# Taking the 512 token columns of a matmul in another order: runs of 4 to 128 columns, alternating between two halves

## The chip, the cores and the metric

The kernel runs on one core of a Trainium2 chip. A core has a matrix engine (TensorE, PE in the profile, with its weight loads listed apart as PEld), VectorE (DVE), ScalarE (ACT), GpSimd (POOL) and SyncE (SP, which issues the DMAs here). Matmuls read their operands from SBUF and write sums into PSUM, which has banks of 512 fp32 columns for each of 128 partitions. The metric is the device time of one execution in microseconds; less is better.

## The reference

A streaming encoder of two layers on one sequence of 512 tokens and 1,024 features, all fp32:

```python
def swiglu(h, w_in, w_out):
    gate, up = jnp.split(h @ w_in, 2, axis=-1)
    return (jax.nn.silu(gate) * up) @ w_out

def reference(x, ...):
    for l in range(DEPTH):                       # DEPTH = 2
        x = x + 0.5 * swiglu(rms_norm(x, ffn1_norm[l]), ffn1_w_in[l], ffn1_w_out[l])
        x = x + hybrid_mixer(rms_norm(x, mix_norm[l]), ...)
        x = x + 0.5 * swiglu(rms_norm(x, ffn2_norm[l]), ffn2_w_in[l], ffn2_w_out[l])
    return rms_norm(x, final_norm)
```

`w_in` is 1024 x 5632 (gate and up), `w_out` is 2816 x 1024. The mixer is a projection, three groups of heads (a convolution, stick-breaking attention, retention) and a projection back. The change concerns only the last product of `swiglu`, here called the outward product.

## The kernel before

Activations lie feature-major: a tile is 128 features (partitions) by 512 tokens (columns), so `x` is eight tiles. A weight block of 128 x 128 is the stationary operand of a matmul, a tile of activations the moving one, and the result, 128 output features by 512 tokens, fills one PSUM bank.

To keep fp32 accuracy each operand is split into a rounded part and a rest, `hi` and `lo`, both of type fp32r. Weights arrive by DMA (`w_raw`), ScalarE casts them (L347) and VectorE subtracts (L350). `product` (L357 to L374) then makes three matmuls for each block of 128 input features: hi x hi (L368), hi x lo (L369) and lo x hi (L370), all summed into one bank `acc`. `self.pe` puts two blocks, six matmuls, into one step of the plan.

`ffn` handles the 2,816 hidden features as 22 tiles in three parts, `PARTS` = tiles 0 to 7, 8 to 15 and 16 to 21. For each hidden tile of a part it makes the gate sums `pg` and the up sums `pu` (eight blocks each, so 24 matmuls each), and `gated` turns them into the split pair `hh`, `hl` on VectorE and ScalarE (L476 to L480, L315, L318). When a part's tiles are there, the outward products run: for each of the eight output tiles d, `po` sums over the part's 8, 8 or 6 hidden tiles, so 24, 24 or 18 matmuls. VectorE scales `po` into `t` (L502) and adds that to `x[d]` (L507). Over the four FFNs each output tile d takes 4 x 22 x 3 = 264 outward matmuls.

The order on every queue comes from a planner. Each step is given a cost (for a group of matmuls the number of columns times `COLUMN`), a list of what it reads and writes and, in the mixer, a delay. The planner plays all engines forward in time and writes the steps out in the order in which they start. So outward products of one part stand among the first gate and up products of the next. PSUM has three banks for `pg`, `pu`, `po` and the projections.

One product elsewhere matters for reading the profile. In the stick-breaking heads `scores` adds a mask to the diagonal blocks of a bank of scores. Where the bank holds two such blocks it does so in one matmul, whose output is a view of two pieces and whose moving operand is the same 128 columns twice (L655):

```python
diag = z[:].rearrange("p (a b) -> p a b", b=P)[:, 0 : 3 * n - 2 : 3, :]
mm(
    diag, self.ident_r[:], self.mask[:, None, :].to_broadcast([P, n, P]), start=False, stop=True,
```

The retention heads run the same `scores` without the mask. `weighted` (L676) multiplies weights with values in plain slices of 512, 384, 128 and 256 columns, and `values` (L607 to L609) makes value tiles in plain slices of 512 or 256 columns; the values are then written to SBUF in pieces of 64 columns, hi and lo in turn (L621, L625).

Of the kernel before, what the change touches and what calls it, by code (L numbers as in the profile page):

```python
# [27 lines left out]
N_RAW = 3  # L28

DENSE_LATE, TAPS_LATE = 200, 400  # L30
PARTS = ((0, 8), (8, 16), (16, 22))
TT = S // P

# [42 lines left out]
class Plan:  # L76
# [167 lines left out]
    def order(self):  # L244
        self.link()
        self.total = self.forward([o.i + o.late for o in self.ops])
        return sorted(self.ops, key=lambda o: (o.start, o.i))
# [42 lines left out]
class Kernel:  # L290
# [63 lines left out]
            )  # L354
        return hi, lo

    def product(self, acc, w, rhs, ks, first=True, last=True, step=2):  # L357

        mm = self.nc.tensor.matmul
        hi, lo = w  # L360
        for a in range(0, len(ks), step):
            some = ks[a : a + step]

            def fn(a=a, some=some):
                for i, (k, m) in enumerate(some):
                    c = slice(k * P, (k + 1) * P)
                    h, l = rhs[m]
                    mm(acc[:], hi[:, c], h[:], start=first and a + i == 0, stop=False)  # L368
                    mm(acc[:], hi[:, c], l[:], start=False, stop=False)  # L369
                    mm(acc[:], lo[:, c], h[:], start=False, stop=last and a + i == len(ks) - 1)  # L370

            self.pe(
                len(some) * 3 * S * COLUMN, fn, [hi, lo, *(t for _, m in some for t in rhs[m])], [acc], self.late
            )  # L374
# [94 lines left out]
    def ffn(self, w_in, w_out, after, first=None):  # L469
        nc = self.nc  # L470
        ks = [(k, k) for k in range(KT)]

        def gated(pg, pu, hs):
            rstd = self.rstd
            g, s, u = (self.tile(self.f2, n) for n in "gsu")
            self.v(S, lambda: nc.vector.tensor_tensor(out=g[:], in0=pg[:], in1=rstd[:], op=ALU.mult), [pg, rstd], [g])  # L476
            self.last_silus = [
                self.a(S, lambda: nc.scalar.activation(s[:], g[:], ACT.Silu), [g], [s], "silu")
            ]
            self.v(S, lambda: nc.vector.tensor_tensor(out=u[:], in0=pu[:], in1=s[:], op=ALU.mult), [pu, s], [u])  # L480
            self.split(u, S, *hs)

        pg, pu = self.products(first or [self.weight(w_in[0, i], KT) for i in range(2)], self.mm)
        self.norm(self.y)
        for a, b in PARTS:
            n = b - a
            hs = [(self.tile(self.r2, "hh", dtype=F32R), self.tile(self.r2, "hl", dtype=F32R)) for _ in range(n)]
            for f in range(a, b):
                if f:
                    pg = self.bank(self.mm, "pg")  # L490
                    self.product(pg, self.weight(w_in[f, 0], KT), self.xs, ks)
                    pu = self.bank(self.mm, "pu")
                    self.product(pu, self.weight(w_in[f, 1], KT), self.xs, ks)
                gated(pg, pu, hs[f - a])
            for d in range(KT):
                po = self.bank(self.mm, "po")
                self.product(po, self.weight(w_out[d][:, a:b, :], n), hs, ks[:n])
                t = self.tile(self.f2, "t")
                x, rstd = self.x[d], self.rstd
                self.v(  # L500
                    S,
                    lambda t=t, po=po, rstd=rstd: nc.vector.scalar_tensor_tensor(  # L502
                        out=t[:], in0=po[:], scalar=0.5, in1=rstd[:], op0=ALU.mult, op1=ALU.mult
                    ),
                    [po, rstd], [t],
                )
                self.v(S, lambda t=t, x=x: nc.vector.tensor_tensor(out=x[:], in0=x[:], in1=t[:], op=ALU.add), [x, t], [x], 2)  # L507
                if b == NF:
                    after(d)
# [641 lines left out]
```

## Time and profile before

| what | value |
|---|---|
| time, median of two runs | 2012.01 us (2010.58 to 2013.43) |
| the profiled execution's own time | 2009.54 us |
| its span, first to last instruction | 2007.7 us |
| PE busy | 1955.3 us (97%), 8,930 matmuls |
| DVE busy / ACT busy | 1094.5 us (55%) / 753.6 us (38%) |
| mean granted TensorE clock | 0.991 |
| outward matmuls `po` | 3 groups (L368, L369, L370) of 704 |

Spans, busy times and waits are those of one profiled execution. A group's row gives its busy time, the mean duration of one instruction in ns, and the idle time of its engine just before it, with what ended that idle time. Matmuls overlap in the pipeline, so the duration of one is longer than its distance to the next.

### The profile page before, as it was taken

The page shows a single profiled execution, that of the slowest core. Times are in us where ns is not written, and L with a number is a line of the kernel's source. Part 1 is how long each engine was busy: PE and PEld are TensorE (multiplying, and loading weights), DVE is VectorE, ACT ScalarE, POOL GpSimd, SP SyncE. Part 2 cuts the span into 40 slices and gives each one's busy share as a digit, 9 for nine tenths or more (in the row PEclk, how much of TensorE's full clock was granted, in tenths as well). Part 3 has the DMA queues.
Part 4 walks back from the last instruction along what each step waited for, and adds up shares of the span by engine and source line. Part 5 has one row for each costly group of instructions (what it writes and reads, how often), then busy time and mean ns, then how long its engine had stood idle before and what let it go on. Part 6 is the DMA issues. An engine that isn't in the chain of part 4 may idle for free.

```text
span 2007.7 us, 22494 instructions
## 1 busy us (share of the span) xinstructions
PE 1955.3 (97%) x8930; PEld 1619.5 (81%) x8930; DVE 1094.5 (55%) x1505; ACT 753.6 (38%) x1096; POOL 20.3 (1%) x21
## 2 busy tenths in 40 slices
PE   8999999999988999999999999999999799999997
PEld 6888888888867888888888888888887588888885
DVE  5443433768996444444643444456699954444445
ACT  5322223564955322223422222236559543222132
POOL 0000000000000000000000000000000000000000
PEclk9999999999999999999999999999999899999998
DMA  6323232432213232332323323223321133233221
GB/s 206 101 90 104 85 104 77 125 94 90 58 42 105 86 104 95 94 104 84 98 95 98 101 94 104 90 78 117 94 85 51 49 111 96 93 105 95 95 89 58
DMA packets 60777, 187.95 MB, mean 94 GB/s; under 512 B 8320, under 2 KB 8832, under 8 KB 60544
## 3 DMA queue, kind: packets, MB, share of 16 engines
q1 hardware_dynamic: 60672, 186.52, 29.8%
q8 instruction: 70, 1.15, 0.2%
q14 instruction: 35, 0.29, 0.0%
HBM read 176.00 MB, written 2.10 MB: 89 GB/s over the span
## 4 chain that ended last, share of the span: by engine, by line
PE 76%; issue 18%; DVE 4%; ACT 1%; DMA 0%; POOL 0%; SPq 0%; POOLq 0%; DVEq 0%; ACTq 0%
PE po L369 6%; PE po L370 6%; PE po L368 6%; PE pu L368 6%; PE pg L370 6%; PE pg L369 6%; PE pu L369 6%; PE pg L368 6%; PE pu L370 6%; PE pj L368 3%; PE pj L370 3%; PE pj L369 3%; PE z L726 2%; DVE yc L890 1%; PE z L648 1%
## 5 line engine op out<-in xcount | busy, mean ns | idle before, releaser
L347 ACT CAST w_hi<-w_raw 128x1024 fp32r<-128x1024 f32 (+2 forms) x354 | 349.5, 989 | 1027.8 <-PE po L369 298.6
L350 DVE TENSOR_TENSOR w_lo<-w_raw,w_hi 128x1024 fp32r<-128x1024 f32 (+2 forms) x354 | 402.0, 1143 | 42.0 <-ACT w_hi L347 31.4
L480 DVE TENSOR_TENSOR u<-pu,s 128x512 f32<-128x512 f32 x84 | 58.1, 692 | 491.3 <-PE pu L370 491.3
L370 PE MATMUL po<-hh,w_lo 128*128 128x512 f32 x704 | 273.9, 389 | 0.0
L369 PE MATMUL po<-hl,w_hi 128*128 128x512 f32 x704 | 273.9, 389 | 0.0
L368 PE MATMUL po<-hh,w_hi 128*128 128x512 f32 x704 | 273.9, 389 | 0.0
L368 PE MATMUL pg<-xh,w_hi 128*128 128x512 f32 x672 | 263.2, 392 | 0.0
L368 PE MATMUL pu<-xh,w_hi 128*128 128x512 f32 x672 | 261.6, 389 | 0.1
L370 PE MATMUL pg<-xh,w_lo 128*128 128x512 f32 x672 | 261.5, 389 | 0.0
L369 PE MATMUL pg<-xl,w_hi 128*128 128x512 f32 x672 | 261.4, 389 | 0.0
L370 PE MATMUL pu<-xh,w_lo 128*128 128x512 f32 x672 | 261.4, 389 | 0.0
L369 PE MATMUL pu<-xl,w_hi 128*128 128x512 f32 x672 | 261.4, 389 | 0.0
L502 DVE SCALAR_TENSOR_TENSOR t<-po,rstd 128x512 f32<-128x512 f32 x96 | 66.3, 691 | 202.4 <-PE po L370 202.3
L368 PEld LDWEIGHTS po<-hh,w_hi 128*128 128x128 f32 x704 | 132.2, 188 | 27.5
L369 PEld LDWEIGHTS po<-hl,w_hi 128*128 128x128 f32 x704 | 132.2, 188 | 27.5
L370 PEld LDWEIGHTS po<-hh,w_lo 128*128 128x128 f32 x704 | 132.1, 188 | 27.3
L369 PEld LDWEIGHTS pg<-xl,w_hi 128*128 128x128 f32 x672 | 126.2, 188 | 27.1 <-issue 1.0
L368 PEld LDWEIGHTS pu<-xh,w_hi 128*128 128x128 f32 x672 | 126.1, 188 | 27.1 <-DVE g L476 0.9
L368 PEld LDWEIGHTS pg<-xh,w_hi 128*128 128x128 f32 x672 | 126.2, 188 | 27.0 <-issue 1.0
L369 PEld LDWEIGHTS pu<-xl,w_hi 128*128 128x128 f32 x672 | 126.2, 188 | 26.2
L370 PEld LDWEIGHTS pg<-xh,w_lo 128*128 128x128 f32 x672 | 126.1, 188 | 26.1
L370 PEld LDWEIGHTS pu<-xh,w_lo 128*128 128x128 f32 x672 | 126.2, 188 | 26.1
(149 smaller groups left out, 2565.0 us busy)
## 6 DMA issues: line engine op xcount, KB each, us to landing
w_raw<-in_f_in SPq DMA_DIRECT2D x174, 512.0 KB, 3.3
w_raw<-in_f_out SPq DMA_DIRECT2D x64, 512.0 KB, 3.5
w_raw<-in_m_in SPq DMA_DIRECT2D x36, 512.0 KB, 3.4
w_raw<-in_f_out SPq DMA_DIRECT2D x32, 384.0 KB, 3.1
w_raw<-in_m_out SPq DMA_DIRECT2D x32, 256.0 KB, 3.0
w_raw<-in_m_vs SPq DMA_DIRECT2D x8, 512.0 KB, 3.4
qh<-qh SPq DMA_DIRECT2D x24, 128.0 KB, 2.2
ql<-ql SPq DMA_DIRECT2D x24, 128.0 KB, 2.8
```

Source lines behind the costliest of these rows:

```text
L347: self.a(m, lambda c=c: nc.scalar.copy(hi[:, c], raw[:, c]), [at(raw)], [at(hi)])
L350: lambda c=c: nc.vector.tensor_tensor(out=lo[:, c], in0=raw[:, c], in1=hi[:, c].bitcast(F32), op=ALU.subtract),
L368: mm(acc[:], hi[:, c], h[:], start=first and a + i == 0, stop=False)
L369: mm(acc[:], hi[:, c], l[:], start=False, stop=False)
L370: mm(acc[:], lo[:, c], h[:], start=False, stop=last and a + i == len(ks) - 1)
L480: self.v(S, lambda: nc.vector.tensor_tensor(out=u[:], in0=pu[:], in1=s[:], op=ALU.mult), [pu, s], [u])
L502: lambda t=t, po=po, rstd=rstd: nc.vector.scalar_tensor_tensor(out=t[:], in0=po[:], scalar=0.5, in1=rstd[:], op0=ALU.mult, op1=ALU.mult),
L648: mm(z[:, c : c + n], k[:, kt * P : (kt + 1) * P], q[i][:, kt * P :], start=kt == tiles[0][0] and i == 0, stop=end and i == 1,)
L726: nc.tensor.matmul(z[:, c : c + n], m[:], logs[jb][part][:, jc : jc + n], start=False, stop=i == len(todo) - 1 and part == 1, skip_group_c ...
L890: nc.vector.scalar_tensor_tensor(out=y[:], in0=v, scalar=w, in1=y[:], op0=ALU.mult, op1=ALU.add)
```

## The change

`product` gets an argument `turns`. With 1, the operands are whole tiles as before. With b > 1, the output bank and both moving operands are passed as the same rearranged view of 512 columns: the columns are cut into two halves (tokens 0 to 255 and 256 to 511), each half into pieces of b columns, and the view takes a piece of the first half, a piece of the second, the next piece of the first and so on. As output and moving operand are taken in the same order, each token's result stands in the column where it stood before. `ffn` passes `TURNS[d]` for the outward products alone, by output tile: 1 for tile 0, then 4, 8, 16, 32, 64, 128 and, for tile 7, 16.

```diff
+TURNS = (1, 4, 8, 16, 32, 64, 128, 16)
...
-    def product(self, acc, w, rhs, ks, first=True, last=True, step=2):
+    def product(self, acc, w, rhs, ks, first=True, last=True, step=2, turns=1):
...
+        def order(t):
+            return t[:] if turns == 1 else t[:].rearrange("p (a n b) -> p n a b", a=2, b=turns)
...
-                    mm(acc[:], hi[:, c], h[:], start=first and a + i == 0, stop=False)
-                    mm(acc[:], hi[:, c], l[:], start=False, stop=False)
-                    mm(acc[:], lo[:, c], h[:], start=False, stop=last and a + i == len(ks) - 1)
+                    mm(order(acc), hi[:, c], order(h), start=first and a + i == 0, stop=False)
+                    mm(order(acc), hi[:, c], order(l), start=False, stop=False)
+                    mm(order(acc), lo[:, c], order(h), start=False, stop=last and a + i == len(ks) - 1)
...
-                self.product(po, self.weight(w_out[d][:, a:b, :], n), hs, ks[:n])
+                self.product(po, self.weight(w_out[d][:, a:b, :], n), hs, ks[:n], turns=TURNS[d])
```

## The prediction
> **What bounds the kernel now.** I read the page of the profile first, for the engine that is never free.
>
> ```profile
> span 2007.7 us, 22494 instructions
> ...
> PE 1955.3 (97%) x8930; PEld 1619.5 (81%) x8930; DVE 1094.5 (55%) x1505; ACT 753.6 (38%) x1096; POOL 20.3 (1%) x21
> ...
> PE   8999999999988999999999999999999799999997
> ...
> PEclk9999999999999999999999999999999899999998
> ```
>
> TensorE is busy for 97% of the span. Its slices fall under 9 only at the start, around slices 12 and 32 (the ends of the two mixers) and at the very end, and the granted clock is at 0.9 or more in all slices but one. VectorE and ScalarE have 45% and 62% of the span to spare. Busy PE time alone doesn't say that the array is the limit, so the second view is the busy time of each engine in four stretches that hold the outward products `po`, the only instructions that the change touches.
>
> ```profile
> core 0: us, PE busy (x) PEld busy (x) DVE busy (x) ACT busy (x) POOL busy (x), PEclk, DMA share, GB/s
> 96.00:140.00 44.00, 44.00 (x195) 36.44 (x195) 19.86 (x25) 9.02 (x10) 0.00 (x0) 1.00 0.33 100
> 335.00:376.00 41.00, 41.00 (x182) 33.94 (x181) 29.33 (x42) 20.24 (x29) 0.00 (x0) 1.00 0.34 104
> 1846.00:1890.00 44.00, 44.00 (x196) 36.44 (x195) 20.26 (x25) 9.20 (x10) 0.00 (x0) 1.00 0.27 84
> 1953.00:1990.00 37.00, 37.00 (x165) 30.56 (x163) 20.39 (x30) 9.73 (x15) 0.00 (x0) 1.00 0.16 43
> ```
>
> In all four PE is busy for the whole stretch at clock 1.00, and no other engine is over 83% (PEld) or 72% (DVE). The third view is the groups by line.
>
> ```profile
> L370 PE MATMUL po<-hh,w_lo 128*128 128x512 f32 x704 | 273.9, 389 | 0.0
> L369 PE MATMUL po<-hl,w_hi 128*128 128x512 f32 x704 | 273.9, 389 | 0.0
> L368 PE MATMUL po<-hh,w_hi 128*128 128x512 f32 x704 | 273.9, 389 | 0.0
> ...
> L502 DVE SCALAR_TENSOR_TENSOR t<-po,rstd 128x512 f32<-128x512 f32 x96 | 66.3, 691 | 202.4 <-PE po L370 202.3
> L368 PEld LDWEIGHTS po<-hh,w_hi 128*128 128x128 f32 x704 | 132.2, 188 | 27.5
> ```
>
> No `po` product ever found PE idle (0.0 in the last column of all three). VectorE, which takes `po` out of PSUM, is the one that waits: 202.3 us for PE. The weight load takes 188 ns and then has a gap, 27.5 us over 704 loads or 39 ns each, so 227 ns from one load to the next.
>
> The mean of 389 ns is a latency, since neighbours overlap. What a product costs is the distance between starts. From the order of time in the first FFN, these are the first and the last of 1,059 starts of `pg`, `pu` and `po` products in a row.
>
> ```profile
> 100.13 0.39 PE L368 MATMUL pu<-xh,w_hi 128*128 128x512 f32 x1
> ...
> 339.95 0.39 PE L370 MATMUL pu<-xh,w_lo 128*128 128x512 f32 x1
> ```
>
> 239.82 us over 1,058 distances is 226.7 ns per product, with `po` and `pu` alike. So every nanosecond added to a `po` product is added to the span, and nothing hides it.
>
> **The change part by part.** *What is touched.* 704 x 3 = 2,112 `po` products, 264 for each of the eight output tiles. Tile 0 has a turn of 1 and stays as it is. The other seven are 1,848 products, at 226.7 ns together 418.9 us, a fifth of the span.
>
> *What is added.* Each of them still writes 512 columns and reads 512 columns, in another order: pieces of b columns, one from tokens 0 to 255, one from 256 on, in turn. That is 512/b pieces in place of one run, 128, 64, 32, 16, 8, 4 and 32 for the tiles 1 to 7, so 127 + 63 + 31 + 15 + 7 + 3 + 31 = 277 jumps over the seven, each with 264 products: 73,128 jumps, on the reading side (h, l in SBUF) and the writing side (`po` in PSUM) at once.
>
> *What stays.* No instruction comes or goes and no wait is added. The output goes through the same order as the input, so each token's sum stands in its own column, and VectorE reads `po` as a plain row as before. The planner is given the same cost for each group, so the orders of all queues (weight loads on SP, casts on ScalarE, subtractions on VectorE) are the same list. All of this costs nothing even without cover, since it doesn't change.
>
> *What a jump costs* is the one unknown. The trace has one matmul form with a jump: the mask product of the stick-breaking heads (L655), whose 256-column form writes two pieces of 128 columns, 0 to 127 and 384 to 511 of a bank, and reads the same 128 columns twice, so that reading jumps too. It stands behind two 128-column products on the same bank. In the retention heads, which have no mask, a plain 256-column product stands at the same place. First the masked head, then the plain one, each with the product before and the one behind:
>
> ```profile
> 517.00 0.27 PE L648 MATMUL z<-ql,kk 128*128 128x128 f32 x1
> 517.11 0.33 PE L655 MATMUL z<-r_mask,ident_r 128*128 128x256 f32 x1
> 517.28 0.39 PE L368 MATMUL pj<-xh,w_hi 128*128 128x512 f32 x1
> ```
>
> ```profile
> 444.65 0.27 PE L648 MATMUL z<-ql,kk 128*128 128x128 f32 x1
> 444.76 0.33 PE L648 MATMUL z<-qh,kk 128*128 128x256 f32 x1
> 444.94 0.28 PE L648 MATMUL z<-ql,kk 128*128 128x256 f32 x1
> ```
>
> Start to start, the product with the jump takes 0.17 us, the one without 0.18. Over all such, from the groups by line with shapes kept apart (the `y` product also follows two 128-column ones; the `pv` rows are wanted for the columns):
>
> ```profile
> L608 PE MATMUL pv<-w_hi,xl 128*128 128x512 f32 x64 | 25.0, 390 | 0.0
> ...
> L608 PE MATMUL pv<-w_hi,xl 128*128 128x256 f32 x64 | 18.1, 283 | 0.0
> ...
> L676 PE MATMUL y<-wh,vs 128*128 128x256 f32 x16 | 5.4, 334 | 0.0
> ...
> L655 PE MATMUL z<-r_mask,ident_r 128*128 128x256 f32 x16 | 5.3, 332 | 0.0
> ```
>
> 332 against 334 ns: one jump costs -2 ns, nothing within what the rows resolve, and I take 2 ns either way as the bound. Upward that is 73,128 x 2 ns = 146 us. Downward a better limit holds: the `pv` rows give (390 - 283)/256 = 0.418 ns per column, so 512 columns need 214.0 of the 226.7 ns, and an order of columns can at best win the other 12.7 ns: 1,848 x 12.7 = 23.5 us.
>
> Pieces under 128 columns don't occur on PE in this trace. The nearest rows are VectorE's, which writes `vs` in pieces of 64 (every other 64 columns of SBUF) and `xl` as a plain row with the same operation:
>
> ```profile
> L398 DVE SCALAR_TENSOR_TENSOR xl<-x,c_gains,xh 128x512 fp32r<-128x512 f32 x48 | 35.6, 748 | 7.1 <-ACT xh L395 7.0
> ...
> L625 DVE SCALAR_TENSOR_TENSOR vs<-pv,rt,vs 128x512 fp32r<-128x512 f32 x8 | 6.0, 746 | 1.3 <-ACT vs L621 1.3
> ```
>
> 746 against 748 ns with seven jumps: no price for a jump on that side either, though on a slower engine. Between 0 and 2 ns per jump I take 0, the value that both pairs of rows are nearest to.
>
> *The sum*: 1,848 x 0 ns on the path, nothing elsewhere. The profiled execution took 2009.5 us with a span of 2007.7; the two timed runs have a median of 2012.0, 2.5 us above it. I forecast 2,011 us, between the two.
>
> The Trainium skill has two rules on this. PSUM — Partial Sum Buffer, section Specifications (TRN2), says of PSUM's 8-byte lines that any access pattern that isn't contiguous slows matmuls significantly; the mask product above isn't contiguous and doesn't show it, and if the rule held in that form the time would be the one of the third rival. Advanced Engine Details and Errata, section Memory Cachelines, asks less: two accesses to each 16-byte line of SBUF and each two neighbouring columns together in PSUM, which pieces of 4 fp32 columns satisfy, so by that section the sum stays as it is; no run here shows pieces that short on PE.
>
> **The rivals.** *1. Each jump costs a little.* The pair of rows resolves 2 ns, but a price of one column's time, 0.418 ns, would slip under it, and 73,128 x 0.418 = 30.6 us gives about 2,041 us. Two columns' time, 0.836 ns, is 61.1 us, 2,072 us. For: the jumps are many and PE has no slack. Against: both pairs came out at -2 ns, and 334 ns would have become 334.4, which they can't deny. It turns to slower by over 2% (40 us) at 0.55 ns per jump. I give 0.05 to the part below that point and 0.08 to the part above.
>
> *2. Only the shortest pieces cost (the rival on the slow side with one place).* Pieces of 4 columns (tile 1, 264 products) lie 256 columns apart, so that a fetch of a few neighbouring columns serves one piece and the next fetch goes elsewhere. If such a product ran at half the pace, 264 x 226.7 ns = 59.8 us, 2,071 us; if pieces of 8 did as well, 119.7 us, 2,131 us. It decides from a pace of 1.67 times in tile 1 (40 us). For: nothing under 128 was seen. Against: four columns still lie side by side. Chance 0.08.
>
> *3. Any break halves the pace.* All 1,848 products at 453 ns: 418.9 us, about 2,430 us. Against it stands the mask product, broken and no slower; what is left is that a break in reading to a far column, or a third free dimension, counts and that one didn't. Chance 0.04. This is the rule of PSUM — Partial Sum Buffer in the Trainium skill, taken at its word.
>
> *4. The order helps.* Up to 23.5 us, so 1,987 to 2,009 us. No row speaks for it. Chance 0.02.
>
> That the change doesn't do what it says is hardly possible: with two halves in turn no two pieces are neighbours, so the rows can't be merged back into one.
>
> **How the numbers follow.** No change has 0.73. That case alone spans 2,003 to 2,017 us: the profiled run and the two timed ones lie within 4 us, and I allow twice that. The range reaches from 2,003 to 2,042 us, which takes in the first rival up to one column's time per jump (0.05) and part of the fourth, about 0.8 in all; the 2 ns bound is left out, since its upper half would need a price that the mask product should have shown. Chances by 2% either side, about what a measurement of this kernel can tell from no change: slower 0.08 + 0.08 + 0.04 = 0.20; faster 0.01, since the limit of 23.5 us is 1.2%; within 2% the remaining 0.79.
>
> **What would show it right or wrong.** The distance between starts is the whole test. In the third part of each FFN (335 us on in the first) the eight tiles follow one another with 18 products each, so about 4.1 us of `po` for each piece length. If all eight show 226.7 ns, the main step holds. If the distance grows with the number of jumps, about in the ratio 127, 63, 31, 15, 7, 3, the first rival holds; if only tile 1 stretches, the second; if all but tile 0 stretch alike, the third. VectorE's wait for `po` (202.3 us) should stay if PE keeps its pace and grow if it doesn't. A changed granted clock, or PE idle before `po`, would mean that something happened that I didn't consider.

## The result, and the profile after

The changed kernel took 2,037.41 us (median of two runs, 2,036.81 to 2,038.02) against 2,012.01: a ratio of 1.0126 [1.0083, 1.017], so it is slower by about 25 us, inside the forecast range and within 2%, but beyond what the runs scatter. The page of the changed kernel, its head and the shares by engine:

```profile
span 2035.0 us, 22504 instructions
...
PE 1982.5 (97%) x8930; PEld 1625.8 (80%) x8930; DVE 1096.1 (54%) x1505; ACT 754.2 (37%) x1096; POOL 20.3 (1%) x21
...
PEclk9999999999999999999999999999999899999998
```

The span grew by 27.3 us (2,035.0 against 2,007.7) and PE's busy time by 27.2 (1,982.5 against 1,955.3), with as many matmuls and the other engines within 2 us. The time is all on PE. The groups by line say in which products (lines stand six further down than before; the last numbers of a row are busy us, mean ns, idle us before and its releaser):

```profile
L375 PE MATMUL po<-hl,w_hi 128*128 128x512 f32 x704 | 281.6, 400 | 0.0
L376 PE MATMUL po<-hh,w_lo 128*128 128x512 f32 x704 | 281.5, 400 | 0.0
L374 PE MATMUL po<-hh,w_hi 128*128 128x512 f32 x704 | 281.1, 399 | 0.0
...
L508 DVE SCALAR_TENSOR_TENSOR t<-po,rstd 128x512 f32<-128x512 f32 x96 | 66.3, 691 | 222.3 <-PE po L376 221.3
```

The three groups of `po` hold 844.2 us where they held 821.7: 22.5 us more. VectorE waits 221.3 us for them where it waited 202.3. The other 4.7 us of PE lie outside `po`. The mean granted TensorE clock differs between the two profiled runs, first before, then after:

```profile
core 0: 2007.7 us, clock 0.991
core 0: 2035.0 us, clock 0.988
```

2,035 x 0.003 is about 6 us, an estimate from three digits, and enough for the 4.7. The change need not be the cause: 30 runs of the kernel before beside the experiments lie between 2,008.5 us at clock 0.992 and 2,017.2 at 0.984, with a median of 2,013.4 us and of 0.988, the clock of the changed kernel's run.

The test that the prediction named is the distance between starts. In the third part of the first FFN the timeline has the output tiles one after another, the first three and the last two of them in turn by steps of six products. The rows are start (us), latency (us), engine, line, product; the first seven open stretches with pieces of 4, 8, 16, 32, 64, 128 and 16, and the eighth is the product behind six of the last.

```profile
353.36 0.41 PE L374 MATMUL po<-hh,w_hi 128*128 128x512 f32 x1
...
354.86 0.41 PE L374 MATMUL po<-hh,w_hi 128*128 128x512 f32 x1
...
356.32 0.40 PE L374 MATMUL po<-hh,w_hi 128*128 128x512 f32 x1
...
360.64 0.40 PE L374 MATMUL po<-hh,w_hi 128*128 128x512 f32 x1
...
364.90 0.40 PE L374 MATMUL po<-hh,w_hi 128*128 128x512 f32 x1
...
369.00 0.39 PE L374 MATMUL po<-hh,w_hi 128*128 128x512 f32 x1
...
370.36 0.40 PE L374 MATMUL po<-hh,w_hi 128*128 128x512 f32 x1
...
371.80 0.40 PE L374 MATMUL po<-hh,w_hi 128*128 128x512 f32 x1
```

From row to row there are 6, 6, 18, 18, 18, 6 and 6 products, so the distances are 250, 243, 240, 237, 228, 227 and 240 ns. Over all 264 products of each form, start to start in the whole trace:

| pieces of | jumps | distance, ns | over 226.7 | per jump |
|---|---|---|---|---|
| 512 (tile 0) | 0 | 228.1 | 1.4 | |
| 4 | 127 | 252.2 | 25.5 | 0.20 |
| 8 | 63 | 243.1 | 16.4 | 0.26 |
| 16 (tiles 3 and 7) | 31 | 240.4 | 13.7 | 0.44 |
| 32 | 15 | 236.5 | 9.8 | 0.65 |
| 64 | 7 | 228.2 | 1.5 | 0.21 |
| 128 | 3 | 228.2 | 1.5 | 0.5 |

Their sum is (1.4 + 25.5 + 16.4 + 2 x 13.7 + 9.8 + 1.5 + 1.5) x 264 = 22.0 us, which is what the groups show. The 1.4 and 1.5 ns of the last forms and of tile 0 aren't theirs alone: untouched products right behind turned ones stretch too. These are the starts of the first of six plain `pu` products behind turned ones and of the product that follows them:

```profile
346.14 0.40 PE L374 MATMUL pu<-xh,w_hi 128*128 128x512 f32 x1
...
347.54 0.41 PE L374 MATMUL po<-hh,w_hi 128*128 128x512 f32 x1
```

1.40 us over six is 233 ns in place of 226.7.

### The profile page after: what moved, and what is told of

Same layout as the page of the kernel before. It is cut to its first block, busy times and chain, and to the rows that moved or that the text cites. A ratio compares the mean times of both kernels' runs of the same rounds, so it can differ in the third digit from the quotient of the medians.

```text
span 2035.0 us, 22504 instructions
## 1 busy us (share of the span) xinstructions
PE 1982.5 (97%) x8930; PEld 1625.8 (80%) x8930; DVE 1096.1 (54%) x1505; ACT 754.2 (37%) x1096; POOL 20.3 (1%) x21
## 4 chain that ended last, share of the span: by engine, by line
PE 76%; issue 18%; DVE 3%; ACT 1%; POOL 0%; DMA 0%; POOLq 0%; DVEq 0%; SPq 0%; ACTq 0%
PE po L376 6%; PE po L375 6%; PE po L374 6%; PE pu L374 6%; PE pg L375 6%; PE pg L376 6%; PE pu L375 6%; PE pg L374 6%; PE pu L376 6%; PE pj L374 3%; PE pj L376 3%; PE pj L375 3%; PE z L732 2%; DVE yc L896 1%; PE z L654 1%
## 5 line engine op out<-in xcount | busy, mean ns | idle before, releaser
L375 PE MATMUL po<-hl,w_hi 128*128 128x512 f32 x704 | 281.6, 400 | 0.0
L376 PE MATMUL po<-hh,w_lo 128*128 128x512 f32 x704 | 281.5, 400 | 0.0
L374 PE MATMUL po<-hh,w_hi 128*128 128x512 f32 x704 | 281.1, 399 | 0.0
L508 DVE SCALAR_TENSOR_TENSOR t<-po,rstd 128x512 f32<-128x512 f32 x96 | 66.3, 691 | 222.3 <-PE po L376 221.3
L374 PEld LDWEIGHTS pu<-xh,w_hi 128*128 128x128 f32 x672 | 126.1, 188 | 27.3 <-DVE g L482 0.9
```

The source lines that it names most:

```text
L374: mm(order(acc), hi[:, c], order(h), start=first and a + i == 0, stop=False)
L375: mm(order(acc), hi[:, c], order(l), start=False, stop=False)
L376: mm(order(acc), lo[:, c], order(h), start=False, stop=last and a + i == len(ks) - 1)
```

## The experiments

Diffs are against the changed kernel unless another is named. Where a kernel was timed once, it stands beside runs of the kernel before with the median of 2,013.4.

**Reading or writing?** The first run turns the moving operands alone, the second the output alone.

Of the three products the second is shown, the others are edited alike.

```diff
-                    mm(order(acc), hi[:, c], order(l), start=False, stop=False)
+                    mm(acc[:], hi[:, c], order(l), start=False, stop=False)
```

```diff
-                    mm(order(acc), hi[:, c], order(l), start=False, stop=False)
+                    mm(order(acc), hi[:, c], l[:], start=False, stop=False)
```

> Only the moving operands (h, l in SBUF) are taken in turns, the output bank is written as a plain row; so the sums of a token land in another token's column, which changes no amount of work. In the changed kernel the distance between starts of outward products was 252 ns with pieces of 4, 243 with 8, 240 with 16, 237 with 32, and 228 with 64 and 128. Theory A, the price is on the reading side: the same six distances, time about 2,037 us. Theory B, the price is on the writing side: 226.7 to 228 ns with all pieces, about 2,012 us. Theory C, both sides pay and the prices add: distances between the two, and what is missing is found in the run with the writing side alone.

> Only the output bank in PSUM is written in turns, the moving operands are read as plain rows; again tokens land in other columns and the work is the same. Theory A (reading side): 226.7 to 228 ns with all pieces, about 2,012 us. Theory B (writing side): 252, 243, 240, 237, 228, 228 ns, about 2,037 us. Theory C: the rest of what the run with the reading side alone showed, so that the two excesses over 226.7 ns add up to those of the changed kernel.

Reading side: 2,037.22 us, 1.0116 [1.0097, 1.0135]. Writing side: 2,013.42 us, 0.9998 [0.9989, 1.0008]. The groups of the first:

```profile
L376 PE MATMUL po<-hh,w_lo 128*128 128x512 f32 x704 | 281.5, 400 | 0.0
...
L508 DVE SCALAR_TENSOR_TENSOR t<-po,rstd 128x512 f32<-128x512 f32 x96 | 66.3, 691 | 222.6 <-PE po L376 221.8
```

And of the second:

```profile
L376 PE MATMUL po<-hh,w_lo 128*128 128x512 f32 x704 | 273.9, 389 | 0.0
...
L508 DVE SCALAR_TENSOR_TENSOR t<-po,rstd 128x512 f32<-128x512 f32 x96 | 66.3, 691 | 202.3 <-PE po L376 202.3
```

The first has the changed kernel's latency and VectorE's wait, and by form its distances are those of the table to 0.1 ns; the second has the numbers of the kernel before. The whole loss lies in the order in which h and l are read. The ten more instructions of the changed kernel (22,504 against 22,494), semaphores on PE, came with the turned output and not with the turned reading; they cost nothing.

**Long pieces alone.** Tile 0 stays plain, the others take pieces of 64 and 128.

```diff
-TURNS = (1, 4, 8, 16, 32, 64, 128, 16)
+TURNS = (1, 64, 128, 64, 128, 64, 128, 64)
```

> Pieces of 64 and 128 columns alone (tile 0 plain, then 64, 128, 64, 128, 64, 128, 64). Theory step: pieces of 64 and more cost nothing by themselves, the 228 ns seen beside slower products come from those; 226.7 ns in all tiles and about 2,012 us, no difference from before. Theory per jump: the 25.4 us of the changed kernel over 73,128 jumps are 0.35 ns each; here are 4 x 7 + 3 x 3 = 37 jumps x 264 = 9,768, so 3.4 us, about 2,015 us, and 229.2 ns with pieces of 64.

2,013.95 us, 1.0005 [0.9995, 1.0014], and distances of 226.7 to 227.0 ns. Pieces of 64 and more are free by themselves, so the 1.5 ns of the table came from their neighbours. A price per jump would have shown; there is a step between 64 and 32 columns instead.

**Shorter pieces, and other distances between them.** A turn is now a pair (parts, piece): the 512 columns are cut into so many parts, each into pieces, and a piece of each part is taken in turn. (2, b) is the form of the change; (16, 16) steps 32 columns from piece to piece, (64, 4) steps 8.

```diff
-TURNS = (1, 4, 8, 16, 32, 64, 128, 16)
+TURNS = ((2, 2), (4, 16), (8, 16), (16, 16), (32, 16), (16, 4), (64, 4), None)
...
-            return t[:] if turns == 1 else t[:].rearrange("p (a n b) -> p n a b", a=2, b=turns)
+            return t[:] if turns is None else t[:].rearrange("p (a n b) -> p n a b", a=turns[0], b=turns[1])
```

> Both sides in turn as in the changed kernel, but the row is cut into more parts than two, so that a jump goes less far. Tile 0: two halves in pieces of 2 (255 jumps of 256 columns). Tiles 1 to 3: pieces of 16 from 4, 8 and 16 parts, jumps of 128, 64 and 32 columns, 31 jumps each. Tile 4: 32 parts of 16, which is the plain order again. Tiles 5 and 6: pieces of 4 from 16 and from 64 parts, jumps of 32 and of 8 columns, 127 jumps each. Tile 7 plain. Theory number of jumps: 240 ns for tiles 1 to 3 and 252 for 5 and 6, whatever the distance; tile 0 above 252. Theory distance: the excess of 13 ns (pieces of 16) and 25 ns (pieces of 4) falls as the jump gets shorter, to nothing at 8 columns. Tiles 4 and 7: 226.7 to 228 by both.

2,057.53 us. In its timeline these are the first of six products with pieces of 2 and the product behind them, then the first of 18 with (16, 4) and the product behind those:

```profile
343.91 0.50 PE L374 MATMUL po<-hh,w_hi 128*128 128x512 f32 x1
...
345.93 0.41 PE L374 MATMUL pu<-xh,w_hi 128*128 128x512 f32 x1
...
371.08 0.40 PE L374 MATMUL po<-hh,w_hi 128*128 128x512 f32 x1
...
375.51 0.40 PE L374 MATMUL po<-hh,w_hi 128*128 128x512 f32 x1
```

2.02 us over six is 337 ns: pieces of 2 cost half as much again as the plain product. (16, 4) takes 246 ns. Over all products (4, 16) takes 234.6, (8, 16) 238.7, (16, 16) 239.6 and (64, 4) 232.6 ns. The distance counts beside the length: of these five forms the two with 127 jumps each are the dearest, (16, 4), and the cheapest, (64, 4). To have that without changing neighbours, a later run gave each FFN one form for all its tiles, with the same view:

```diff
-TURNS = (1, 4, 8, 16, 32, 64, 128, 16)
+TURNS = ((4, 16), (16, 16), (16, 4), (64, 4))
...
-                self.product(po, self.weight(w_out[d][:, a:b, :], n), hs, ks[:n], turns=TURNS[d])
+                self.product(po, self.weight(w_out[d][:, a:b, :], n), hs, ks[:n], turns=TURNS[self.ffns - 1])
```

> Both sides in turn, one order per FFN: pieces of 16 columns from 4 parts (jumps of 128 columns), pieces of 16 from 16 parts (32 columns), pieces of 4 from 16 parts (32 columns), pieces of 4 from 64 parts (8 columns). Theory number of pieces: 240 ns twice and 250 ns twice, as with two halves, 528 x (13.3 + 13.3 + 23.3 + 23.3) ns = 38.7 us more, about 2,052 us. Theory distance matters too: about 235, 240, 246 and 233 ns, as these orders had among others in one kernel, 528 x (8 + 13 + 19 + 6) ns = 24 us more, about 2,037 us.

2,039.49 us. The third part of the first and of the third FFN, 126 products each:

```profile
345.58 0.39 PE L374 MATMUL po<-hh,w_hi 128*128 128x512 f32 x1
...
374.72 0.39 PE L374 MATMUL pf<-xh,w_hi 128*128 128x512 f32 x1
```

```profile
1355.09 0.40 PE L374 MATMUL po<-hh,w_hi 128*128 128x512 f32 x1
...
1386.17 0.40 PE L374 MATMUL pf<-xh,w_hi 128*128 128x512 f32 x1
```

29.14 / 126 = 231.3 ns for (4, 16), 31.08 / 126 = 246.7 for (16, 4); the steady middle of the other two gives 240.0 for (16, 16) and 231.1 for (64, 4).

**Each length by itself.** One for each FFN, in the form of the change.

```diff
-TURNS = (1, 4, 8, 16, 32, 64, 128, 16)
+TURNS = (4, 8, 16, 32)
...
+                self.product(po, self.weight(w_out[d][:, a:b, :], n), hs, ks[:n], turns=TURNS[self.ffns - 1])
```

> Both sides in turn, all eight output tiles of an FFN with one piece length: 4 in the first FFN, 8 in the second, 16 in the third, 32 in the fourth, so that slow products have slow neighbours of their own kind. Theory each form has its own price, whatever the neighbours: 252, 243, 240 and 236.5 ns, that is 528 x (25.5 + 16.3 + 13.4 + 9.8) ns = 34.3 us over before, about 2,047 us. Theory the prices come from the switches between orders: less than half of that, under 2,030 us.

2,052.36 us. The third parts of the first three FFNs:

```profile
354.42 0.41 PE L374 MATMUL po<-hh,w_hi 128*128 128x512 f32 x1
...
385.93 0.40 PE L374 MATMUL pf<-xh,w_hi 128*128 128x512 f32 x1
```

```profile
994.09 0.40 PE L374 MATMUL po<-hh,w_hi 128*128 128x512 f32 x1
...
1024.74 0.40 PE L374 MATMUL pf<-xh,w_hi 128*128 128x512 f32 x1
```

```profile
1364.21 0.40 PE L374 MATMUL po<-hh,w_hi 128*128 128x512 f32 x1
...
1394.45 0.39 PE L374 MATMUL pf<-xh,w_hi 128*128 128x512 f32 x1
```

31.51, 30.65 and 30.24 us over 126 are 250.1, 243.3 and 240.0 ns; pieces of 32 have 236.7 in steady stretches. So each length has a price of its own, and the neighbours only blur it. 528 x (23.3 + 16.6 + 13.3 + 10.0) ns = 33.4 us over 2,013.4 is 2,047 us; for the 5 us beyond that, the granted clock of this run is lower, 0.984 against the median of 0.988 of the kernel before, and 2,050 x 0.004 is about 8 us, an estimate.

**Do two halves of a product pay it too?** Each product is cut into two of 256 columns, with tile 0 plain, then pieces of 4, 8, 16, 32, 64 in turn from two parts of the 256 (so 128 columns apart), and two more plain tiles; `cut` is 2 and `order` takes the part that begins at `at`.

```diff
+                    for w, r in ((hi, h), (hi, l), (lo, h)):
+                        for at in range(0, S, S // cut):
+                            begin = first and a + i == 0 and w is hi and r is h and at == 0
+                            mm(order(acc, at), w[:, c], order(r, at), start=begin, stop=end and w is lo, **kw)
```

> Each outward product is cut into two of 256 columns, and the turns are taken inside each 256: tile 0 plain, then pieces of 4, 8, 16, 32 and 64 columns from two parts that lie 128 columns apart, tiles 6 and 7 plain. Plain products of 256 columns had 0.12 us from start to start in the heads of the kernel before. Theory per product (a product whose reading jumps loses a fixed time at its start, about 13 ns, and very short pieces a little more): the excess over plain is about the same for 256 columns as for 512, 13 ns with pieces of 16 and 10 with 32. Theory per piece (each jump costs): it is half, 6 to 7 ns with pieces of 16, 5 with 32, 12 to 13 with 4.

2,049.12 us. The first two rows enclose 36 products with pieces of 16, the next two 72 plain ones (the last row is the first product of the projection behind the FFN):

```profile
359.82 0.40 PE L380 MATMUL po<-hh,w_hi 128*128 128x256 f32 x2
...
364.14 0.40 PE L380 MATMUL po<-hh,w_hi 128*128 128x256 f32 x2
...
372.72 0.40 PE L380 MATMUL po<-hh,w_hi 128*128 128x256 f32 x2
...
381.36 0.40 PE L380 MATMUL pf<-xh,w_hi 128*128 128x512 f32 x1
```

120.0 ns with and without pieces of 16; over all products 127.3 with pieces of 4, 123.3 with 8, 119.3 with 32 and 119.8 plain. Two plain halves cost 240 ns, 13 more than one whole product, and within that room pieces of 16 and 32 are hidden. Neither theory foresaw a pace in which the plain product itself has slack; only pieces of 4 and 8 still show.

**Is it the weight load?** A load of 188 ns runs beside every product. Here all products but the first of each sum use 64 of the 128 weight columns (`cols`), and `half` is the output's first 64 partitions.

```diff
-                    mm(order(acc), hi[:, c], order(l), start=False, stop=False)
+                    mm(half(acc), hi[:, c][:, :cols], order(l), start=False, stop=False, **kw)
```

> As the changed kernel, but after the first product of each sum only 64 of the 128 weight columns are loaded and used, so output rows 64 to 127 miss all later products; the moving side is the same. Theory weight load (the jumping reads lose time because the load of the next weights reads SBUF beside them): with a load of half the length the excess over plain falls to about half, 12 to 13 ns with pieces of 4 and 6 to 7 with 16. Theory reading alone: the excess stays, 25, 16, 13 and 10 ns with pieces of 4, 8, 16 and 32.

2,034.54 us. The groups of one of the three products and of its load:

```profile
L383 PE MATMUL po<-hh,w_lo 128*64 128x512 f32 x704 | 281.0, 399 | 0.0
...
L383 PEld LDWEIGHTS po<-hh,w_lo 128*64 128x64 f32 x704 | 95.3, 135 | 71.5
```

The load fell from 189 to 135 ns, by 29% and not by half, and the mean product only from 400 to 399. By form: 248.1, 242.0, 240.4, 234.5 ns for pieces of 4 to 32. But the forms that were free rose. These are the first of 18 products with pieces of 64 and the product behind them:

```profile
365.72 0.39 PE L379 MATMUL po<-hh,w_hi 128*128 128x512 f32 x1
...
369.86 0.39 PE L379 MATMUL po<-hh,w_hi 128*128 128x512 f32 x1
```

4.14 us over 18 is 230.0 ns, and over all products tile 0 and pieces of 64 and 128 take 230.0, 229.9 and 229.7 ns. Against that, the excess is 18, 12, 10 and 4.5 ns for pieces of 4 to 32. Against 226.7 it is 21, 15, 14 and 8. A price in proportion to the load, 135/189 of 25, 16, 13 and 10 ns, would be 18, 11, 9 and 7, so this run does not decide between the two theories: half the price shows in neither count for pieces of 4 to 16, and a part of the load in it isn't excluded.

**Bytes or columns?** All operands of the dense products, `hh` and `hl` among them, are kept as bf16 pairs in place of fp32r; the second run, against the kernel before, has no turns.

```diff
-            hs = [(self.tile(self.r2, "hh", dtype=F32R), self.tile(self.r2, "hl", dtype=F32R)) for _ in range(n)]
+            hs = [(self.tile(self.r2, "hh", dtype=BF16), self.tile(self.r2, "hl", dtype=BF16)) for _ in range(n)]
```

> As the changed kernel, but all split operands of the dense products (weights, inputs, hidden tiles, mixer outputs) are bf16 in place of fp32r, so a column has 2 bytes in place of 4 and the splits keep fewer digits. The reading side had its step between pieces of 32 columns (128 bytes, 10 ns) and 64 columns (256 bytes, nothing). Theory bytes: the step is at 256 bytes again, so pieces of 128 columns are free and pieces of 64 and 32 columns pay, and pieces of 4 columns (8 bytes) pay about what pieces of 2 fp32 columns paid (110 ns over plain). Theory columns: the step is at 64 columns again, pieces of 64 and 128 are free, and pieces of 4 pay about 25 ns.

> The bf16 kernel with all outward products in the plain order, against the kernel before (fp32r, plain order); the splits keep fewer digits than fp32r's. In the bf16 kernel with turns a plain product took 215.8 ns, pieces of 8 to 128 columns 216, and pieces of 4 columns 227. Theory bf16 reads at half the bytes and has time to spare: only the 264 products with pieces of 4 get faster, by 11 ns each, 3 us, so about 1,929 us. Theory the turns cost elsewhere in bf16 too: more than 10 us less than the 1,932 us with turns.

With turns 1,932.43 us, without them 1,929.21, 0.9583 [0.9567, 0.9599] of the kernel before: the fastest kernel here, at the price of fewer digits in each split. From the run with turns, six products with pieces of 4 and six with pieces of 8, each from its first to the next product:

```profile
326.45 0.39 PE L375 MATMUL po<-hh,w_hi 128*128 128x512 bf16 x1
...
327.81 0.38 PE L375 MATMUL pu<-xh,w_hi 128*128 128x512 bf16 x1
...
330.46 0.38 PE L375 MATMUL po<-hh,w_hi 128*128 128x512 bf16 x1
...
331.76 0.38 PE L375 MATMUL po<-hh,w_hi 128*128 128x512 bf16 x1
```

227 ns and 217 ns, where a plain bf16 product takes 215.8. Pieces of 4 pay 11 ns, all longer ones nothing. Neither theory holds as stated, for pieces of the same length in bytes or in columns have other prices: at 8 bytes fp32r pays 110 ns (337 - 227), bf16 11; at 8 columns fp32r pays 16, bf16 nothing.

**Shorter pieces in PSUM.** Output side alone, one form for each FFN: pieces of 2 and of 4 from two halves, pieces of 4 and of 2 in steps of 8 columns.

```diff
-TURNS = (1, 4, 8, 16, 32, 64, 128, 16)
+TURNS = ((2, 2), (2, 4), (64, 4), (64, 2))
...
+                    mm(order(acc), hi[:, c], l[:], start=False, stop=False)
```

> Only the output bank in PSUM is written in turns, the moving operands are plain rows (so tokens land in other columns, the work is the same), with one order per FFN: pieces of 2 columns from two halves in the first FFN, of 4 from two halves in the second, of 4 that step by 8 columns in the third, of 2 that step by 8 columns in the fourth. Theory the writing side is free: 226.7 ns in all four, about 2,013 us. Theory writing has a rate of its own that shorter pieces reach, as reading has: more than 226.7 ns in the first and fourth FFN, 240 ns there would be 2 x 528 x 13.3 ns = 14 us more.

2,014.84 us:

```profile
L376 PE MATMUL po<-hh,w_lo 128*128 128x512 f32 x704 | 273.9, 389 | 0.0
```

389 ns and 226.7 from start to start in all four forms. Down to two columns the order of writing costs nothing.

**Other places in SBUF.** Pieces of 4, 16, 32 and 64, one for each FFN, with the raw weight slots 32 columns wider, so that the tiles behind them move.

```diff
-        raw = self.tile(self.raw, "w_raw", (P, KT * P))
+        raw = self.tile(self.raw, "w_raw", (P, KT * P + 32))
```

> Both sides in turn with two halves, one piece length per FFN (4, 16, 32, 64), and the slots of w_raw are made 32 columns wider, which moves every hidden tile in SBUF by 384 bytes: their rows began 128 bytes past a multiple of 256 bytes and now begin on one. Theory place: the step between pieces of 32 columns (128 bytes) and 64 columns (256 bytes) comes from where the pieces lie against some boundary, so with the new base pieces of 32 or 64 columns have another price than 236.7 and 226.7 ns. Theory piece length: 250, 240, 236.7 and 226.7 ns as before, 528 x (23.4 + 13.3 + 10) ns = 24.7 us more than before, about 2,038 us.

2,075.33 us, 37 more than any theory gave. The distances up to 32 were unmoved (250.0, 240.0, 236.7 ns); what had changed was a product that nobody had turned:

```profile
L374 PE MATMUL po<-hh,w_hi 128*128 128x512 f32 x704 | 283.7, 403 | 0.0
...
L375 PE MATMUL pu<-xl,w_hi 128*128 128x512 f32 x672 | 265.3, 395 | 0.0
```

395 ns for `pu` where it was 389, and 232.8 from start to start; pieces of 64 had 232.4. So six kernels with plain order followed, based on the kernel before, with only the places of its tiles changed: raw slots 32, 64, 16 and 96 columns wider; then a tile of 32 columns ahead of everything; then that together with raw slots 32 wider. The edit of the last one holds both kinds:

```diff
+        pad = self.tile(room("pad", 1), "pad", (P, 32))
+        plan.add("vector", vec(32, 0), lambda: nc.vector.memset(pad[:], 0.0), [], [pad])
         self.whi, self.wlo = (room(n, N_W) for n in ("w_hi", "w_lo"))
...
-        raw = self.tile(self.raw, "w_raw", (P, KT * P))
+        raw = self.tile(self.raw, "w_raw", (P, KT * P + 32))
```

The first expectation speaks of two raw slots; there are three, so the tiles behind them moved by 384 B.

> The kernel before, with the two raw weight slots 32 columns (128 B) wider each, so that the tiles behind them, the moving operands among them, lie further on in SBUF; the order of the columns is plain everywhere, nothing is left out. Theory place: the place of the moving tile alone sets the pace of a plain product, so all of them start about 232.8 ns apart as the plain ones beside the turned ones did in the run with moved tiles, and the run takes about 2,013 + 8,900 x 6.1 / 1,000 = 2,067 us. Theory neighbours: they were slow only because turned products ran among them; distances 226.7 ns and 2,013 us.

> The same with 64 columns (256 B) more in each raw slot, plain order, nothing left out. Theory place: the tiles are moved by 256 B x 2 or so against the weight block; if only the equal phase of before is good, about 232.8 ns and 2,067 us; if the good places repeat after 512 B or less, 226.7 ns and 2,013 us. Theory neighbours: 226.7 ns and 2,013 us.

> The same with 16 columns (64 B) more in each raw slot, plain order, nothing left out. Theory place: another phase of the moving tile against the weight block; between 220 and 233 ns, the run between 1,955 and 2,067 us, and a distance below 226.7 ns would be a place better than that of the kernel before. Theory neighbours: 226.7 ns and 2,013 us.

> The same with 96 columns (384 B) more in each raw slot, plain order, nothing left out. Theory place: another phase of the moving tile against the weight block; between 220 and 233 ns, the run between 1,955 and 2,067 us. Theory neighbours: 226.7 ns and 2,013 us.

> The kernel before, plain order, with a tile of 32 columns (128 B) put ahead of all others, so that the weight blocks and the moving tiles both lie 128 B further on and keep their distance from each other; nothing is left out. So far moving tiles at 128 B past a multiple of 256 B, with weights at 128 B too, take 226.7 ns, those at 0 take 232.4 ns and those at 64 take 233.3 ns. Theory distance: what counts is the place of the moving tile against the weight block; 226.7 ns and about 2,013 us. Theory own place: what counts is the moving tile's own place past a multiple of 256 B; 232.4 ns and about 2,049 us.

> The same with the tile of 32 columns ahead and 32 columns more in each of the three raw weight slots, so that the weight blocks lie 128 B further on (at 0 past a multiple of 256 B) and the moving tiles stay at 128, plain order; nothing is left out. Theory distance: some 232.4 ns and 2,049 us, since the two differ by 128 B as in the run with 128 B more in each raw slot. Theory own place: 226.7 ns and 2,013 us.

The weight load's row of the third product of `po` in each, in this order (busy and idle time over 704 is the distance from load to load):

```profile
L370 PEld LDWEIGHTS po<-hh,w_lo 128*128 128x128 f32 x704 | 132.6, 188 | 30.9
```

```profile
L370 PEld LDWEIGHTS po<-hh,w_lo 128*128 128x128 f32 x704 | 132.1, 188 | 27.7
```

```profile
L370 PEld LDWEIGHTS po<-hh,w_lo 128*128 128x128 f32 x704 | 132.2, 188 | 32.1
```

```profile
L370 PEld LDWEIGHTS po<-hh,w_lo 128*128 128x128 f32 x704 | 132.7, 189 | 30.8
```

```profile
L370 PEld LDWEIGHTS po<-hh,w_lo 128*128 128x128 f32 x704 | 132.2, 188 | 27.6
```

```profile
L370 PEld LDWEIGHTS po<-hh,w_lo 128*128 128x128 f32 x704 | 132.5, 188 | 31.3
```

| kernel | weights, B past a multiple of 512 | moving tiles, the same | difference, B past a multiple of 256 | load to load, ns | time, us |
|---|---|---|---|---|---|
| before | 128 | 128 | 0 | 226.8 | 2,013.4 |
| raw slots + 32 | 128 | 0 | 128 | 232.2 | 2,048.66 |
| raw slots + 64 | 128 | 384 | 0 | 227.0 | 2,011.55 |
| raw slots + 16 | 128 | 320 | 192 | 233.4 | 2,056.77 |
| raw slots + 96 | 128 | 256 | 128 | 232.2 | 2,049.65 |
| all moved | 256 | 256 | 0 | 227.0 | 2,008.94 |
| weights alone moved | 256 | 128 | 128 | 232.7 | 2,054.58 |

Place counts without any turn (the theory of the neighbours falls), and it is the distance between the two operands that counts, not the moving tile's own place: moving both together costs nothing, and moving either one alone by 128 or 192 B past a multiple of 256 B does. The raw weight slots lie between the two and moved as well; PE doesn't read them, and no run moves them alone. Equal places in steps of 256 B are the good ones of those tried; the kernel before had one, and none here beat it beyond the scatter of its runs (down to 2,008.5 us). The load itself kept its 188 to 189 ns; the idle time between loads grew from 27.5 to 27.7 us at the good places to 30.8 to 32.1. Each of these kernels but the one before was timed once, so the distance, not the time, carries the reading.

## Why the prediction was wrong

*What bounds the kernel* held. PE is the limit and nothing hides a longer `po` product: 22.5 us in the groups of `po` came out as 25 us of the median. (The granted clock stands at 8 in two slices of its row, the 32nd and the last, not in one.)

*What stays* was off by ten semaphore instructions on PE, which cost nothing (the run with the writing side alone has them too and took 2,013.42 us), and right in the rest: PE makes as many matmuls, none of the `po` groups waits (0.0 idle), and VectorE only waits longer for the same product.

*What a jump costs* is the step that failed: "Between 0 and 2 ns per jump I take 0". The value was right for what its rows showed. The mask product reads and writes pieces of 128, and pieces of 64 and 128 are free (226.7 to 227.0 ns with these alone); the order of writing is free down to 2 columns. It was wrong to carry it to reading in pieces of 4 to 32, for which the trace had no row on PE. VectorE's pieces of 64, taken as the nearest row, were of a length that is free on PE too, above the step between 64 and 32, and on another engine. Of the 1,848 products that were costed at nothing, 1,320 (tiles 1 to 4 and 7) paid 10 to 25 ns and 528 (tiles 5 and 6) nothing of their own.

*The rivals.* The first, a small price for each jump, is the nearest in time: 2,041 us at one column's time per jump, against 2,037.4. Its form is wrong. The price per jump runs from 0.20 to 0.65 ns in the table, not in the ratio of the jumps, and jumps between pieces of 64 are free. The second had the right place, short pieces, but a ninth of the size for pieces of 4 (25 ns, not 227), and left out 16 and 32. The third and fourth saw nothing of theirs. The rule of the Trainium skill behind the third, in PSUM — Partial Sum Buffer, section Specifications (TRN2), is contradicted by these runs for writing matmuls: pieces of 2 and 4 columns of PSUM took 226.7 ns. The other one, Advanced Engine Details and Errata, section Memory Cachelines, asks for two accesses to a 16-byte line of SBUF; pieces of 4 fp32r columns at a 16-byte boundary give it four, and paid 23 ns. The prediction said that this section asks less than the first rule; it has the two milder conditions, but on PSUM it repeats the first rule as well, so it did not speak for a sum of 0 as plainly as the prediction has it.

*Range and chances.* The range held the time, and that was luck: its upper end was set by the first rival at one column's time per jump, a price that doesn't exist in that form, and by the case that was given 0.73 the time would have been 2,017 us at most. The chance of 0.73 for no change was too high, since it stood on two pairs of rows none of which had a piece under 64 columns; the case to weigh more was a cost of 10 to 30 ns in a product, a tenth, which neither pair could see.

What stays open is why short pieces cost what they do. A price that goes by the number of jumps alone, by the bytes or by the columns of a piece alone is excluded. The weight load is not: with a shorter load the free forms took 230.0 ns and pieces of 32 went from 236.5 to 234.5. The steady distances of the plain and the two-halves forms (226.7, 236.7, 240.0, 243.3, 250.0) differ by multiples of 3.3 ns, those of 231.1, 231.3 and 232.2 to 232.7 don't fit that. That the distance of the pieces enters (231 to 247 ns for four forms), and that the place of the moving tile against the weights does, makes it plausible that both come from where the reads fall in the memory; that is a guess. So is any cause for the plain products behind turned ones, whose 233 ns is close to the pace of a bad place.

## What to carry to other kernels

Read the moving operand of an fp32r matmul in unbroken pieces of at least 64 columns (free here, taken from two halves); the order of its output in PSUM was free in all forms tried, down to 2 columns, so turn that side instead. A row of the trace bounds an access pattern only down to the piece length that it has: where the change goes below it, keep a cost per product in the sum's bounds (here 4% with pieces of 32, a tenth with 4, a half with 2). And when tiles are added or resized, compare the start distance of products that were not touched, since it depends on where their two operands lie.

## What the runs showed of the hardware that I had not expected

- A plain fp32r product of 512 columns takes 226.7 ns when moving tile and weight block lie a multiple of 256 B apart, and 232 to 233 ns at 128 and 192 B: 35 to 43 us of this kernel.
- Two fp32r products of 256 columns take 240.0 ns, one of 512 takes 226.7.
- With bf16 operands the same product takes 215.8 ns; there reading in pieces of 8 columns or more is free, and pieces of 4 cost 11 ns.
- With a weight load of 135 in place of 189 ns, the products that were free at 226.7 ns took 230.0: a shorter load made them no faster.
